# Twelve small table loads move from ScalarE's DMA queue to SyncE's, behind the pieces of the first modulation

## The chip, the cores and the metric

The kernel runs on one core of a Trainium2 chip. The metric is the device time of one execution, in microseconds (us). The engines are TensorE (PE, with its weight load PEld), VectorE (DVE), ScalarE (ACT), GpSimd (POOL) and SyncE (SP). SP and ACT both issue DMA transfers; the profile shows the issuing instructions as SPq and ACTq. Each engine works through its own instructions strictly in program order.

## The reference, cut to what matters

The program is one inference step of a trunk of two layers over 128 context tokens and 512 latent tokens (five tiles of 128), with a model width of 1024, all in float32:

```python
for l in range(DEPTH):                       # DEPTH = 2
    sh1, sc1, gt1, sh2, sc2, gt2 = split(silu(cond) @ w_ada[l] + b_ada[l], 6)   # for context and latents
    h = rms_norm(x, norm_mix_pre[l]) * (1 + sc1) + sh1
    y = even_mixer(h) if l % 2 == 0 else mla_mixer(h)
    x = x + gt1 * rms_norm(y, norm_mix_post[l])
    ...                                      # squared-ReLU MLP with sh2, sc2, gt2 in the same way
```

Layer 0 is the even mixer: one wide projection `w_in`, then gated linear attention heads and retention heads. The gates are

```python
gate_pre = einsum('bldr,drk->bldk', gk_lr, w_gk2) + b_gk2     # from 2 x 16 columns of the projection
log_a = log_sigmoid(gate_pre) / 16
b = cumsum(log_a within a chunk of 64)                        # positions and a triangle matrix
```

## The kernel before, in words

**Order.** No instruction is placed by hand. Every piece of work is a Python generator (a thread). A planner, `Weave`, keeps a clock for each engine with estimated costs, and each time it gives an engine the ready instruction of the most urgent thread; the resulting order is the program. So an edit of one thread can change the order of the instructions around it on all engines. A number that a thread yields is a pause on the planner's clock, and an `Event` a wait for another thread. `w.aside(...)` issues several loads and goes on.

**Waits of loads.** A load signals its landing on one of eight semaphores (`DMAHW0` to `DMAHW7` in the listings below), which the loads of SP and ACT take in turn. A load waits on its engine until the load before it on the same semaphore has landed. It also waits until its destination is free.

**The start.** `prepare` loads the condition (`cc`, 16 rows) and the identity on SP, and the biases and norms (`vec`, `post`) and the matrix `fold` on ACT. From `cc`, ACT and DVE make silu(cond): an exponential on ACT (`e<-cc`), then a reciprocal and a product on DVE. TensorE transposes it to `cT`, and DVE copies it into `wide`, the stationary operand of all modulation matmuls.

`ada_first` makes the first shift and scale of layer 0 in four quarters of 256 columns each. SP loads their weights as pieces `rada` in an order that `FIRST_LOADS` gives, mixed with the five tiles of `x` and the first four quarters (along the input width) of the first group of `w_in`, `raw` (480 columns). The pieces of the first two quarters are 128x4x256 (0.52 MB each, four to a quarter); those of the last two are 128x2x256 (0.26 MB, eight to a quarter) and take slots of the pools `sv` and `sg`, which the mixer uses later. For each quarter TensorE multiplies the pieces by `wide` into `ps`, ACT copies the sums to `row`, four small matmuls with `fold` turn them, and DVE makes `mod` from them. When all pieces of the four quarters are issued, the event `self.loaded` is set. Three things wait for it: the further weights of `w_in`, the modulation pieces of the next sections (128x512, 0.26 MB), and a part of `make_tables`.

`pre_norm` makes, for every tile and quarter, `xn`, its transposes into a PSUM bank (`ps`), `h` = scale and shift (half on DVE, half on ACT), and `hT` in two parts for the matmuls (ACT's cast and DVE's difference). `gemm_first` multiplies all tiles by the first group of columns of `w_in` (`pg<-wh,hT` and so on), quarter after quarter as they come. `gemm_nat` then goes through the further groups; the second one has 256 columns, and its weights are `wp`.

**`make_tables`** loads what the gates need: the weights and biases of the gates (`wf`, zeroed first by POOL; six loads of 16x4x64 and four of 1x4x64), the positions (`pos`), and the triangle tables (`dist`, 128x256). From them ACT makes `wg` (two casts, with a difference on DVE) and `tri`, and sets `tables`, for which each tile's thread waits after its first group of columns. After `self.loaded` it loads the masks, the decay rates (`lg`, `lgs`) and what else the retention heads need.

All instructions go through one helper line, so the profile names line 271 for all of them; the tiles tell them apart.

Of the kernel before, what the change touches and what calls it, by code (L numbers as in the profile page):

```python
# [33 lines left out]
C_ID, C_TF, C_TB, C_DF, C_DB, C_MF, C_MB, C_DT, C_COS, C_SIN, C_POS, C_FOLD = (  # L34
    0, 128, 256, 384, 512, 640, 768, 896, 1024, 1152, 1280, 1288)
# [298 lines left out]
class Trunk:  # L334
# [1195 lines left out]
    def even(self, ph, ready):  # L1530
        nc, io, w = self.nc, self.io, self.w
# [4 lines left out]
        con = io["consts"]  # L1536
        w.set(self.early, (sv, sg))
        tl = lambda nm, shape, dt=F32: pe.tile(shape, dt, tag=nm, name=nm)
        tri, pos = tl("tri", [P, 256], F32R), tl("pos", [P, 8])
# [11 lines left out]

        def make_tables():

            a = nc.scalar
            wf, hwf = yield from self.take(sg, [98, NH, 2, 64], F32, "wf")
            nc.gpsimd.memset(wf, 0.0)
            nc.gpsimd.memset(ones[96:98], 1.0)
            dist, hd = yield from self.take(sg, [P, 512], F32, "dist")

            loads = [lambda: a.dma_start(pos, con[:, C_POS:C_POS + 8]),  # L1560
                     lambda: a.dma_start(dist[:, 0:256], con[:, C_TF:C_TF + 256])]
            for d in range(2):
                for r in (0, 32, 64):
                    loads.append(lambda d=d, r=r: a.dma_start(
                        wf[r + d * 16:r + d * 16 + 16, :, d], io["w_gk2"][0, d].rearrange("r (h c) -> r h c", h=NH)))
                for r in (96, 97):
                    loads.append(lambda d=d, r=r: a.dma_start(
                        wf[r:r + 1, :, d], io["b_gk2"][0:1, d].rearrange("o (h c) -> o h c", h=NH)))
            there = Event()
            w.aside(*loads, then=lambda at: w.set(there, None, at))  # L1570
            yield there

            wf_ = wf.rearrange("p h d c -> p (h d c)")
            nc.scalar.copy(wg, wf_)
            nc.vector.tensor_sub(wg[64:98], wf_[64:98], wg[64:98].bitcast(F32))
            nc.scalar.copy(wg[96:97], wf_[96:97])
            self.drop(hwf)
            nc.scalar.copy(tri, dist[:, 0:256])
            nc.vector.tensor_copy(pos16, pos[:, 2:4])
            for s in gkT:  # L1580
                nc.vector.tensor_copy(s[96:98], ones[96:98])
            w.set(tables)
            yield self.loaded
            yield 2.0
            dt, hdt = yield from self.take(self.rows, [P, P], F32, "dt")
            e0, h0 = yield from self.take(self.rows, [P, P], F32, "e0")
            e1, h1 = yield from self.take(self.rows, [P, P], F32, "e1")
            nc.sync.dma_start(dist, con[:, C_DF:C_DF + 512])
            nc.vector.tensor_copy(masks, dist[:, 256:512].rearrange("p (a i) -> p a i", a=2))
            w.set(masked)  # L1590
            nc.sync.dma_start(rtab, con[:, C_COS:C_COS + 256].rearrange("p (a t c) -> p a t c", a=2, c=32))
            nc.sync.dma_start(gn, io["gla_norm"][0].partition_broadcast(P))
            nc.sync.dma_start(lg, io["ret_decay"].rearrange("o d h -> (o d h)").partition_broadcast(P))
            for d in range(2):
                nc.sync.dma_start(lgs[d * 64:d * 64 + 64], io["ret_decay"][0, d].partition_broadcast(64))
            nc.sync.dma_start(dt, con[:, C_DT:C_DT + P])
            w.set(gained)
            yield 20.0
            for s in (lg, lgs):
                nc.scalar.activation(s, s, AF.Exp)  # L1600
                nc.vector.tensor_scalar(s, s, -1.0, None, op0=ALU.mult)
            for h in range(NH):
                nc.scalar.activation(e0, dist[:, 0:128], AF.Exp, scale=lg[:, h:h + 1])
                nc.scalar.activation(e1, dist[:, 128:256], AF.Exp, scale=lg[:, 4 + h:5 + h])
                nc.vector.tensor_mul(e0, e0, dist[:, 256:384])
                nc.vector.tensor_mul(e1, e1, dist[:, 384:512])
                nc.vector.tensor_add(dmat[:, h], e0, e1)
                nc.scalar.activation(dec_t[:, h], dt, AF.Exp, scale=lgs[:, h:h + 1])
                yield 2.0
            nc.scalar.activation(dec128, lgs, AF.Exp, scale=128.0)  # L1610
            for d in range(2):
                nc.vector.tensor_scalar(kd[:, :, d], lg[:, d * 4:d * 4 + 4], pos[:, d:d + 1], None, op0=ALU.mult)
            nc.scalar.activation(kd, kd, AF.Exp)

            nc.vector.tensor_scalar(kd, kd, 0.125, None, op0=ALU.mult)
            nc.vector.tensor_scalar(dmat, dmat, 0.0625, None, op0=ALU.mult)
            self.drop(hd, hdt, h0, h1)
            w.set(tables2)

        tables2 = Event()  # L1620
        w.spawn(make_tables(), 0.0)
        G = [[Event() for _ in range(NT)] for _ in EVEN_GROUPS]
        kv_ev = {k: [Event() for _ in range(NT)] for k in ("gla", "ret")}
# [800 lines left out]
```

## Time and profile before

| | before |
|---|---|
| median of 3 runs | 1512.07 us (1511.71 to 1513.47) |
| profiled execution, its own time | 1510.94 us |
| its span, first to last instruction | 1508.8 us |
| mean granted clock | 0.997 |
| TensorE busy | 1468.6 us, 97% of the span |
| ScalarE busy | 659.4 us, 44% |
| transfers | 171.45 MB, mean 114 GB/s; the first fortieth of the span 299 GB/s |

Rows of the timeline are: start, length (us), engine, line, operation, output and inputs, shapes, number of instructions; in brackets the engine's idle time before it and what ended it. A DMA row of ACTq or SPq is the time of the issuing instructions, not of the transfer; the time from issue to landing stands in rows of its own.

### The profile page before, as it was taken

What the parts mean: (1) busy time and instruction counts of PE and PEld (TensorE: products, weight loads), DVE (VectorE), ACT (ScalarE), POOL (GpSimd) and SP (SyncE); (2) the same over time, 40 slices, a digit from 0 to 9 for tenths busy, and PEclk for the clock granted to TensorE, in tenths of its full rate; (3) what the DMA queues carried; (4) which work ended last, traced back from release to release, by engine and by line L of the source; (5) the groups of instructions that cost most, each with busy time, mean ns of one, the idle gap of its engine ahead of it and who ended that gap; (6) DMA issues with size and microseconds to landing.
All of it is one profiled execution on the core that took longest, in us unless ns stands there. A gap on an engine that the chain in (4) does not pass through costs nothing.

```text
span 1508.8 us, 23115 instructions
## 1 busy us (share of the span) xinstructions
PE 1468.6 (97%) x8651; PEld 1304.4 (86%) x8651; DVE 1085.8 (72%) x2234; ACT 659.4 (44%) x1543; POOL 114.5 (8%) x133
## 2 busy tenths in 40 slices
PE   4899999999999999999999999999999999999997
PEld 1688888888899899899898899997889989988996
DVE  2663674657677777777869788884765869996777
ACT  3583533546432223223247476664654323332332
POOL 0000200100121121021020100000012000000000
PEclk9999999999999999999999999999999999999999
DMA  9656222143455454354414210113522223432332
GB/s 299 200 168 196 82 75 70 39 132 112 147 159 156 140 147 147 113 148 151 133 45 133 68 29 22 43 44 124 168 84 70 70 71 112 133 119 84 98 101 110
DMA packets 152400, 171.45 MB, mean 114 GB/s; under 512 B 12272, under 2 KB 100960, under 8 KB 152288
## 3 DMA queue, kind: packets, MB, share of 16 engines
q1 hardware_dynamic: 151104, 169.59, 36.6%
q8 instruction: 68, 1.11, 0.3%
q10 hardware_dynamic: 1184, 0.39, 0.1%
q14 instruction: 44, 0.36, 0.1%
HBM read 161.36 MB, written 8.59 MB: 113 GB/s over the span
## 4 chain that ended last, share of the span: by engine, by line
PE 93%; DVE 3%; ACT 2%; DMA 1%; issue 0%; SPq 0%; DVEq 0%; ACTq 0%
PE p L271 57%; PE pg L271 21%; PE ps L271 13%; PE pqk L271 2%; PE pv L271 1%; DMA rada<-in_w_ada 1%; DVE sm L271 0%; DVE y L271 0%; DVE rope L271 0%; DMA x<-in_x_prompt 0%; ACT junk L271 0%; DVE x L271 0%; DMA wf<-in_w_gk 0%; ACT sm L271 0%; ACT hT L271 0%
## 5 line engine op out<-in xcount | busy, mean ns | idle before, releaser
L271 PE MATMUL p<-wh,hid 128*128 128x512 f32 x1280 | 399.3, 390 | 0.0
L271 PEld LDWEIGHTS p<-wh,hid 128*128 128x128 f32 x1280 | 240.3, 188 | 49.4
L271 PE MATMUL p<-hT,wh 128*128 128x256 f32 (+1 forms) x1280 | 279.6, 309 | 0.0
L271 PE MATMUL p<-wl,hid 128*128 128x512 f32 x640 | 249.5, 390 | 0.0
L271 PE MATMUL pg<-wh,hT 128*128 128x512 f32 (+2 forms) x760 | 245.9, 399 | 1.2 <-ACT hT L271 0.9
L271 DVE TENSOR_TENSOR wl<-raw,wh 128x1024 fp32r<-128x1024 f32 (+2 forms) x137 | 165.3, 1209 | 76.0 <-ACT wh L271 70.8
L271 PEld LDWEIGHTS p<-hT,wh 128*128 128x128 f32 x1280 | 214.8, 188 | 0.8
L271 ACT CAST wh<-raw 128x1024 fp32r<-128x1024 f32 (+2 forms) x141 | 144.8, 1033 | 132.1 <-PE p L271 88.4
L271 PE MATMUL p<-hT,wl 128*128 128x256 f32 (+1 forms) x640 | 198.2, 310 | 0.0
L271 PEld LDWEIGHTS pg<-wh,hT 128*128 128x128 f32 x760 | 140.0, 189 | 31.2 <-issue 4.7
L271 DVE SCALAR_TENSOR_TENSOR ada<-rada,cT,ada 128x512 f32<-128x512 f32 x196 | 146.5, 777 | 0.0
L271 PEld LDWEIGHTS p<-wl,hid 128*128 128x128 f32 x640 | 120.2, 188 | 24.1
L271 DVE TENSOR_TENSOR y<-y,p 128x512 f32<-128x512 f32 x140 | 95.8, 685 | 58.4 <-PE p L271 57.7
L271 POOL TENSOR_TENSOR r<-r 128x384 f32<-128x384 f32 (+1 forms) x80 | 82.4, 1030 | 722.9 <-ACT hid L271 385.4
L271 PE MATMUL pg<-wl,hT 128*128 128x512 f32 (+2 forms) x320 | 130.5, 408 | 0.0
L271 PEld LDWEIGHTS p<-hT,wl 128*128 128x128 f32 x640 | 120.5, 188 | 0.0
L271 ACT ACTIVATE r<-p 128x384 f32<-128x384 f32 (+1 forms) x80 | 35.0, 438 | 152.5 <-PE p L271 152.5
L271 PE MATMUL p<-hT,wq 128*128 128x320 f32 x576 | 88.1, 310 | 0.0
L271 PEld LDWEIGHTS p<-hT,wq 128*128 128x128 f32 x576 | 85.5, 188 | 0.5
L271 DVE TENSOR_TENSOR hid<-r,hid 128x384 fp32r<-128x384 f32 (+1 forms) x80 | 38.9, 487 | 48.8 <-POOL r L271 48.7
L271 PEld LDWEIGHTS pg<-wl,hT 128*128 128x128 f32 x320 | 60.7, 190 | 15.2 <-issue 3.9
L271 ACT CAST wq<-tw 128x512 fp32r<-128x512 f32 x48 | 27.6, 618 | 71.4 <-DVE tw L271 58.1
(290 smaller groups left out, 2384.7 us busy)
## 6 DMA issues: line engine op xcount, KB each, us to landing
raw<-in_w_mlp SPq DMA_DIRECT2D x128, 512.0 KB, 4.1
rada<-in_w_ada SPq DMA_DIRECT2D x176, 256.0 KB, 3.4
raw<-in_w_in_even SPq DMA_DIRECT2D x16, 512.0 KB, 4.5
rada<-in_w_ada SPq DMA_DIRECT2D x8, 512.0 KB, 6.9
x<-in_x_sample SPq DMA_DIRECT2D x8, 512.0 KB, 5.9
gate<-gate SPq DMA_DIRECT2D x8, 512.0 KB, 4.3
raw<-in_w_out_even SPq DMA_DIRECT2D x8, 512.0 KB, 5.0
raw<-in_w_out_odd SPq DMA_DIRECT2D x8, 512.0 KB, 3.9
```

The source lines that it names most:

```text
L271: emit = lambda: real(*a, **k)
```

## The change

`make_tables` now begins with the wait for `self.loaded`, and its twelve first loads are issued by SP. Within them the ten loads of `wf` come first and `pos` and `dist` last; the later `yield self.loaded` is gone. `wf` and `dist` also take their slots only then.

```diff
         def make_tables():
 
-            a = nc.scalar
+            yield self.loaded
             wf, hwf = yield from self.take(sg, [98, NH, 2, 64], F32, "wf")
             nc.gpsimd.memset(wf, 0.0)
             nc.gpsimd.memset(ones[96:98], 1.0)
             dist, hd = yield from self.take(sg, [P, 512], F32, "dist")
 
-            loads = [lambda: a.dma_start(pos, con[:, C_POS:C_POS + 8]),
-                     lambda: a.dma_start(dist[:, 0:256], con[:, C_TF:C_TF + 256])]
+            a = nc.sync
+            loads = []
             for d in range(2):
                 for r in (0, 32, 64):
                     loads.append(lambda d=d, r=r: a.dma_start(
@@ ... @@
+            loads += [lambda: a.dma_start(pos, con[:, C_POS:C_POS + 8]),
+                      lambda: a.dma_start(dist[:, 0:256], con[:, C_TF:C_TF + 256])]
             there = Event()
             w.aside(*loads, then=lambda at: w.set(there, None, at))
             yield there
@@ ... @@
             w.set(tables)
-            yield self.loaded
             yield 2.0
```

What this does to the order, at three places. ScalarE, start of the program, before (`fold` is the last load of `prepare`, `e<-cc` the first arithmetic):

```order
L271 DMA fold<-in_consts 128x128
L271 DMA pos<-in_consts 128x8
L271 DMA dist_159<-in_consts 128x256
L271 DMA wf_154<-in_w_gk 16x4x64 x3
L271 DMA wf_154<-in_b_gk 1x4x64 x2
L271 DMA wf_154<-in_w_gk 16x4x64 x3
L271 DMA wf_154<-in_b_gk 1x4x64 x2
L271 ACTIVATE e_105<-cc_104 16x128
L271 ACTIVATE junk,sm_207<-x_170 128x1024
```

and now:

```order
L271 DMA post_107<-in_norm_mlp_post 16x128
L271 DMA fold<-in_consts 128x128
L271 ACTIVATE e_105<-cc_104 16x128
L271 ACTIVATE junk,sm_206<-x_166 128x1024
L271 ACTIVATE sm_206<-sm_206,eps 128x1
L271 ACTIVATE sm_206<-sm_206 128x1
L271 COPY row_256<-ps_193 128x256
```

The twelve loads between `fold` and `e` are gone. SyncE, from the last pieces of the fourth quarter (128x2x256) on, before, with the waits of each load (`raw` at the end are the weights of the second group of columns):

```order
L271 DMA rada_475<-in_w_ada 128x2x256 [waits DMAHW2_49]
L271 DMA rada_481<-in_w_ada 128x512 [waits DMAHW3_49]
L271 DMA rada_494<-in_w_ada 128x512 [waits DMAHW4_49]
L271 DMA rada_500<-in_w_ada 128x512 [waits DMAHW5_49]
L271 DMA rada_508<-in_w_ada 128x512 [waits DMAHW6_49]
L271 DMA dist_159<-in_consts 128x512 [waits DMAHW7_49,Activation_49]
L271 DMA raw_516<-in_w_in_even 128x2x256 [waits DMAHW0_49,DVE_49]
L271 DMA raw_526<-in_w_in_even 128x2x256 [waits DMAHW1_49,DVE_49]
L271 DMA raw_544<-in_w_in_even 128x2x256 [waits DMAHW2_49,DVE_49,Activation_49]
```

and now, from the last of the four 128x512 pieces on:

```order
L271 DMA rada_499<-in_w_ada 128x512 [waits DMAHW2_49]
L271 DMA wf_473<-in_w_gk 16x4x64 [waits DMAHW3_49,Pool_49]
L271 DMA wf_473<-in_w_gk 16x4x64 [waits DMAHW4_49]
L271 DMA wf_473<-in_w_gk 16x4x64 [waits DMAHW5_49]
L271 DMA wf_473<-in_b_gk 1x4x64 [waits DMAHW6_49]
L271 DMA wf_473<-in_b_gk 1x4x64 [waits DMAHW7_49]
L271 DMA wf_473<-in_w_gk 16x4x64 [waits DMAHW0_49]
L271 DMA wf_473<-in_w_gk 16x4x64 [waits DMAHW1_49]
L271 DMA wf_473<-in_w_gk 16x4x64 [waits DMAHW2_49]
L271 DMA wf_473<-in_b_gk 1x4x64 [waits DMAHW3_49]
L271 DMA wf_473<-in_b_gk 1x4x64 [waits DMAHW4_49]
L271 DMA pos<-in_consts 128x8 [waits DMAHW5_49]
```

The twelve loads (the last, `dist`, follows the last row shown) now stand between these pieces and the weights of the second group. ScalarE, from the copy of the fourth quarter's sums (`row<-ps`) on, before (`h_631` and `h_634` are the fourth quarter of the first tiles):

```order
L271 COPY row_589<-ps_532 128x256
L271 CAST hT_91<-h_578 128x256
L271 CAST hT_91<-h_580 128x256
L271 ACTIVATE h_598<-ps_591,mod_164,mod_165 128x128
L271 CAST hT_91<-h_598 128x256
L271 CAST wp_519<-raw_516 128x512
L271 ACTIVATE h_631<-ps_620,mod_164,mod_165 128x128
L271 CAST wp_575<-raw_526 128x512
L271 ACTIVATE h_634<-ps_621,mod_164,mod_165 128x128
L271 CAST hT_91<-h_631 128x256
```

and now (the fourth quarter of the first tiles is `h_634`, `h_636`, `h_638`):

```order
L271 COPY row_594<-ps_520 128x256
L271 ACTIVATE h_604<-ps_589,mod_160,mod_161 128x128
L271 CAST hT_91<-h_604 128x256
L271 CAST wg_153<-wf_473 98x512
L271 CAST wp_587<-raw_507 128x512
L271 CAST wp_592<-raw_588 128x512
L271 CAST wg_153<-wf_473 1x512
L271 ACTIVATE h_634<-ps_623,mod_160,mod_161 128x128
L271 ACTIVATE h_636<-ps_624,mod_160,mod_161 128x128
L271 CAST wp_600<-raw_593 128x512
L271 ACTIVATE h_638<-ps_625,mod_160,mod_161 128x128
L271 CAST tri<-dist_484 128x256
```

The casts of `wg` and `tri`, which stood among the first and second quarter's work, now stand ahead of and among the fourth quarter's `h`. The order of TensorE, VectorE, GpSimd and SyncE differs through the first half of layer 0 in the same way; from there to the end the instructions come in the same order as before, but for numbers of buffers.

## The prediction

> **What bounds the kernel now.** I read the page's sections 1 and 4 first, then the busy time by windows, then the timeline of the first 60 us, engine by engine. Sections 1 and 4: TensorE is busy for 97% of the span, and the chain that ended last is TensorE for 93% of it.
>
> ```profile
> span 1508.8 us, 23115 instructions
> PE 1468.6 (97%) x8651; PEld 1304.4 (86%) x8651; DVE 1085.8 (72%) x2234; ACT 659.4 (44%) x1543; POOL 114.5 (8%) x133
> PE 93%; DVE 3%; ACT 2%; DMA 1%; issue 0%; SPq 0%; DVEq 0%; ACTq 0%
> ```
>
> So 40 us of the span are TensorE's idle time. The windows (start:end, length, then busy us of PE, PEld, DVE, ACT, POOL, then granted clock, DMA share, GB/s) say where it lies.
>
> ```profile
> 0.00:5.00 5.00, 0.00 (x0) 0.00 (x0) 0.34 (x2) 1.28 (x1) 0.93 (x6) 1.00 0.45 121
> 5.00:10.00 5.00, 0.00 (x0) 0.00 (x0) 0.00 (x0) 0.00 (x0) 0.00 (x0) 1.00 0.86 281
> 10.00:15.00 5.00, 0.00 (x0) 0.00 (x0) 0.00 (x0) 0.00 (x0) 0.00 (x0) 1.00 0.96 306
> 15.00:20.00 5.00, 1.54 (x11) 0.92 (x15) 2.60 (x10) 1.84 (x5) 0.00 (x0) 1.00 0.82 252
> 20.00:25.00 5.00, 4.51 (x36) 1.33 (x26) 0.48 (x1) 0.78 (x2) 0.00 (x0) 1.00 1.03 347
> 25.00:30.00 5.00, 2.74 (x20) 1.27 (x21) 2.70 (x11) 4.06 (x10) 0.00 (x0) 1.00 1.06 375
> 30.00:35.00 5.00, 5.00 (x24) 2.39 (x17) 2.59 (x7) 2.46 (x6) 0.00 (x0) 1.00 1.08 386
> 35.00:40.00 5.00, 3.16 (x22) 2.07 (x22) 3.32 (x10) 3.76 (x9) 0.00 (x0) 1.00 0.60 206
> 40.00:45.00 5.00, 4.64 (x35) 2.68 (x34) 4.29 (x15) 3.29 (x11) 0.00 (x0) 1.00 0.65 199
> 45.00:50.00 5.00, 3.27 (x28) 1.61 (x26) 3.62 (x9) 4.16 (x11) 0.00 (x0) 1.00 0.86 270
> 55.00:60.00 5.00, 5.00 (x35) 3.83 (x34) 2.65 (x10) 3.07 (x8) 0.00 (x0) 1.00 0.46 146
> 200.00:300.00 100.00, 100.00 (x542) 83.03 (x541) 60.77 (x126) 43.63 (x79) 11.38 (x14) 1.00 0.18 53
> ```
>
> TensorE idles for 25 of the first 50 us, most of it before it starts at all; from 55 us on it has none for hundreds of us. What brings that point forward shortens the run by about as much, since the chain behind it is TensorE's own work. The timeline says why the start is late.
>
> ```profile
> 4.00 0.36 ACTq L271 DMA_DIRECT2D fold<-in_consts  x1
> 4.40 0.45 ACTq L271 DMA_DIRECT2D pos<-in_consts  x1
> 14.92 1.31 ACTq L271 DMA_DIRECT2D wf<-in_b_gk  x2
> 16.29 0.31 ACT L271 ACTIVATE e<-cc 16x128 f32<-16x128 f32 x1 [14.27 <-DMA wf<-in_w_gk]
> 19.39 1.94 PE L271 MATMUL ps<-rada,wide 128*32 128x256 f32 x16
> 23.08 1.08 PE L271 MATMUL ps<-rada,wide 128*32 128x256 f32 x8
> 24.23 0.37 ACT L271 COPY row<-ps 128x256 f32<-128x256 f32 x1 [6.03 <-PE ps L271]
> ```
>
> ScalarE (ACT) issues its loads itself, one behind the other, and its first arithmetic, the exponential of the condition (`e<-cc`), stands behind all of them. From 4.40 to 16.23 it is occupied with the twelve loads that the change takes away. Without `e` there is no `cT`, without `cT` no `wide`, and without `wide` no matmul of the modulation (19.39).
>
> **The change part by part.** *The start.* With the twelve loads gone, ACT is free at 4.36, and `e` can begin 11.9 us earlier. The first modulation matmul comes 19.39 − 16.29 = 3.1 us behind it: 7.5 us. But the weights must be there. Up to the last piece of the first quarter, SyncE's queue (SP) brings the identity (0.07 MB), four pieces and one tile of x (0.52 MB each): 2.69 MB. By 5 us 0.6 MB had moved; the other 2.08 MB at 281 GB/s take 7.4 us, so the piece lands at 12.4. A group of four matmuls behind it (1.08) and the copy of the sums to `row` stands at 13.6, against 24.23: 10.6 us earlier. At best it is the full 11.9. At worst the fourth piece, whose issue ended in the trace at 8.3, has the longest landing of its kind:
>
> ```profile
> 5.98 2.34 SPq L271 DMA_DIRECT2D rada<-in_w_ada  x3
> DMA to landing us min/median/max: 2.9/5.5/7.7
> DMA to landing us min/median/max: 3.6/4.0/5.5
> ```
>
> (the first such line is for the modulation pieces up to 60 us, the second for `wf`). That gives 16.0, the copy at 17.2, and 7.0 us. I take 10.6, by the rate that the same queue showed in that stretch.
>
> *Three casts leave the head of ACT.*
>
> ```profile
> 31.97 0.60 ACT L271 CAST wg<-wf 98x512 fp32r<-98x512 f32 x1
> 38.12 0.61 ACT L271 CAST wg<-wf 1x512 fp32r<-1x512 f32 x1
> 39.16 0.40 ACT L271 CAST tri<-dist 128x256 fp32r<-128x256 f32 x1
> ```
>
> The first stood in a gap; the second was directly ahead of the next copy to `row`, the third ahead of the squares of the last tile. Gain 0 to 1.6; I take the 1.0 of the latter two.
>
> *Does the stream keep pace?* Until the last piece of the third quarter 7.77 MB more are needed (8 + 4 halves of a MB in pieces and x, three units of `w_in_even`). At the 369 GB/s of 20 to 35 us that is 21.0 us, landing at 33.4. TensorE used it here:
>
> ```profile
> 46.65 0.64 PE L271 MATMUL ps<-rada,wide 128*32 128x256 f32 x8
> 55.36 0.64 PE L271 MATMUL ps<-rada,wide 128*32 128x256 f32 x8
> 83.19 0.36 PE L271 MATMUL pg<-wp,hT 128*128 128x256 f32 x1
> ```
>
> and now wants it 11.6 earlier, at 35.0: in time. At 306 GB/s it lands at 37.8, 2.8 late. Loss 0 to 2.8; I take 0.5, since 347 to 386 were reached once the queue was full. The last piece of the fourth quarter (2.85 MB on) lands at 41.1 and is wanted at 44.
>
> *What the twelve loads cost on SP.* They stand behind four pieces of the next modulation and ahead of the weights of the second group of output columns. By the order each of them waits for the load eight places before, so the last four of the twelve go out only as the first four land. The four pieces (1.05 MB) have landed at about 44; loads nine to twelve are issued at 44 to 46, and the last of `wf` is there at 49 (4.0, the median). The three weight loads follow by 47.3 and land by 52, taking for them
>
> ```profile
> raw<-in_w_in_even SPq DMA_DIRECT2D x16, 512.0 KB, 4.5
> 50.22 0.62 ACT L271 CAST wp<-raw 128x512 fp32r<-128x512 f32 x1
> 49.87 0.47 ACT L271 ACTIVATE h<-ps,mod,mod 128x128 f32<-128x128 f32 x1
> 65.73 6.32 PE pg L271 x28
> ```
>
> On ACT the cast of `wg`, two casts of these weights and the small cast stand ahead of the last quarter's `h`: two `h` are done at 53.2. They free the banks of PSUM that TensorE needs for the last two tiles' transposes. It comes there 23 matmuls (0.226 each, from the 28 in 6.32), a dozen transposes and the small fold behind the last piece, 7 us after 44.9, at 51.9. So it waits 1.3; I take 1.5. Nothing if the weights land in 3 us; 4.5 if both rounds of landings take the 5.5 that was the longest of `wf`. [...]
>
> At nothing I cost SP's own issue time, twelve times some 0.45 (as `pos` above): from 55 us on the queue is far ahead of TensorE's need (55:60 shows 146 GB/s). That cover goes if the loads of the second group come later than TensorE's first use, 83.19 less the gain. `wf`'s memset on POOL now waits for a slot that a used piece leaves; POOL has nothing else there. The later tables (masks, `lg`, `dt`) are pushed back on SP as well, but their first use on ACT leaves SP until about 78 us to bring them, 30 us behind the twelve loads:
>
> ```profile
> 88.12 0.24 ACT L271 ACTIVATE lg<-lg 128x8 f32<-128x8 f32 x1
> ```
>
> *Sum.* −10.6 − 1.0 + 0.5 + 1.5 = −9.6 us. From 83.19 on the trace shows TensorE without a pause, and from the middle of the first layer the order of all engines is again the same, so I carry all of it to the end: span 1499.2, and with the 2.1 us around it 1501.3 for the profiled execution, which stood 1.1 below the median. Against the median: 1502.5.
>
> **The rivals.** *The stream is the bound and does not move faster.* By 50 us the windows moved 13.7 MB, and the head needs 13.3 and ACT's 0.4: at the old pace the last piece lands at 50, only 5.4 before its old use at 55.36. With the stall that is −4: 1508. For it: 1.0 and more of DMA share at 20 to 35. Against it: 206 and 199 GB/s at 35 to 45, when SP waited for rooms that engines still held, and these now come free earlier:
>
> ```profile
> SPq L271 <- DVE sm L271: 4.4, 1, 4.4
> SPq L271 <- PE ps L271: 4.1, 3, 2.4
> ```
>
> *TensorE starts early but slow.* The same kind of matmul took twice as long early on, though the clock column says 1.00 throughout:
>
> ```profile
> 30.57 0.77 PE L271 MATMUL pg<-wh,hT 128*128 128x480 f32 x1
> 36.18 0.38 PE L271 MATMUL pg<-wl,hT 128*128 128x480 f32 x1
> ```
>
> If it waits for pieces between 8 and 33 us it may stay slow until then: five groups at 1.08 for 0.64 (2.2) and 18 matmuls at twice 0.226 (4.1), less the 3.9 that it idled from 35 to 50: 2.4 lost, 1505. [...]
>
> *The loads block ACT from their new place, and the kernel is slower.* On ACT the twelve took 11.8 us. If they take that on SP from 44 us on, the weights behind them land at 61, the `h` are done at 63.8 and TensorE stands for 11.9: sum +0.8, 1513; with landings of 5.5 for 4.0 it is 16.3 and +5.3, 1517. It decides from a stall of 11.1 us. Against it: on ACT the loads shared the engines with 300 GB/s; behind the last pieces there is 146.
>
> **How the numbers follow.** The forecast has 0.60, the bound stream 0.13 (1508), the slow start 0.12 (1505), the blocked ACT 0.06 (1515), and 0.09 is for a loss by the new order that eats the gain down to less than 3 us. Faster by over 0.2% (3 us, about what can be told here) is then 0.85, within it 0.09, slower 0.06. All bounds together would span 1498.5 (11.9 + 1.6) to 1517; without the last two cases it is 1498.5 to 1508.5.
>
> **What would show it.** In the profile after: `e<-cc` at about 4.5; the copy to `row` at 13 to 14; the first matmul of the second group (`pg<-wp`) at 73 to 74 where it was 83.19; a wait of ACT ahead of `wg<-wf` of some 4 us and a pause of TensorE of one or two near 52. I am wrong if the copy to `row` comes after 17, if TensorE's pause near 52 is over 5, or if the matmul of the second group moves by 10 and the span does not.

## The result, and the profile after

The changed kernel took 1502.38 us (median; 1501.10 to 1502.76), the kernel before, beside it, 1512.77 us (1511.71 to 1513.62): a ratio of 0.9930, with a 95% interval of 0.9916 to 0.9944. The forecast was 1502.5, within 1498.5 to 1508.5. The profiled execution took 1501.1 us. Sections 1 and 4 of its page, which answer to the two lines shown of before:

```profile
span 1499.3 us, 23109 instructions
PE 1470.5 (98%) x8651; PEld 1305.1 (87%) x8651; DVE 1086.4 (72%) x2234; ACT 661.3 (44%) x1543; POOL 114.6 (8%) x133
PE 93%; DVE 3%; ACT 2%; DMA 1%; issue 1%; SPq 0%; DVEq 0%; ACTq 0%
```

TensorE's idle time (span less PE) fell from 40.2 to 28.8 us, by 11.4; its busy time rose by 1.9, with as many matmuls. So the span is 9.5 shorter. Both parts need an explanation. The busy time by windows, in the same columns as before:

```profile
5.00:10.00 5.00, 3.09 (x19) 0.95 (x19) 2.19 (x9) 1.65 (x4) 0.00 (x0) 1.00 1.04 360
10.00:15.00 5.00, 3.79 (x22) 1.62 (x22) 0.38 (x2) 1.54 (x4) 0.00 (x0) 1.00 1.07 370
15.00:20.00 5.00, 2.48 (x18) 0.70 (x18) 3.46 (x11) 3.97 (x11) 0.00 (x0) 1.00 1.09 355
30.00:35.00 5.00, 5.00 (x32) 2.79 (x31) 4.08 (x13) 4.06 (x10) 0.00 (x0) 0.70 1.09 382
```

TensorE now works from 5 us on. The stream moves 355 to 370 GB/s where it had moved 252 to 306: not only ACT but also SP became free (up to 60 us it had waited 7.2 us for landings of `wf`, and now for none). In 30 to 35 the granted clock is 0.70, where before it was 1.00: it stood at half from 29.62 to 33.03. The timeline of the head (ACT, then PE and SP):

```profile
3.77 0.31 ACT L271 ACTIVATE e<-cc 16x128 f32<-16x128 f32 x1 [1.75 <-DMA ident<-in_consts]
13.43 0.37 ACT L271 COPY row<-ps 128x256 f32<-128x256 f32 x1 [4.50 <-PE ps L271]
48.81 0.62 ACT L271 CAST wg<-wf 98x512 fp32r<-98x512 f32 x1
51.85 0.81 ACT L271 ACTIVATE h<-ps,mod,mod 128x128 f32<-128x128 f32 x2
```

```profile
6.43 1.08 PE L271 MATMUL ps<-rada,wide 128*32 128x256 f32 x8 [0.48 <-DVE wide L271]
12.28 1.08 PE L271 MATMUL ps<-rada,wide 128*32 128x256 f32 x8 [0.17 <-DMA rada<-in_w_ada]
45.99 0.64 PE L271 MATMUL ps<-rada,wide 128*32 128x256 f32 x8
53.01 0.27 PE L271 MATMUL ps<-ident,xn 128*128 128x128 f32 x1
67.86 0.28 PE L271 MATMUL pg<-wp,hT 128*128 128x256 f32 x1
```

```profile
39.31 2.00 SPq L271 DMA_DIRECT2D wf<-in_w_gk  x3
44.66 1.30 SPq L271 DMA_DIRECT2D wf<-in_b_gk  x2
46.55 0.36 SPq L271 DMA_DIRECT2D dist<-in_consts  x1
47.01 8.04 SPq L271 DMA_DIRECT2D raw<-in_w_in_even  x6
```

The exponential stands 12.5 us earlier than before (16.29), the first modulation group 13.0 (19.39), the copy to `row` 10.8 (24.23). The twelve loads take SP 7.6 us (39.31 to 46.91). `wg` is cast without a wait, and TensorE comes to the transposes at 53.01 without one.

**A mark for the head.** The first matmul of `pg<-wp` stands 15.3 earlier, but some of the work that stood ahead of it now stands behind it. A mark that has the same work ahead of it in both kernels is the first matmul of layer 0's MLP, with 1970 matmuls ahead in both (the window before counts the mark itself too). Before, then after, the time up to that mark as one window:

```profile
0.00:357.90 357.90, 332.38 (x1971) 263.44 (x1971) 203.06 (x457) 178.98 (x398) 27.32 (x41) 1.00 0.44 140
```

```profile
0.00:345.85 345.85, 332.36 (x1970) 262.99 (x1971) 203.29 (x457) 180.64 (x398) 27.36 (x41) 1.00 0.45 145
```

The head became 12.05 us shorter, all of it idle time of TensorE (25.52 to 13.49). What TensorE waited for up to 55 us, before and then after (us in total, times, longest):

```profile
PE ps L271 <- DMA wf<-in_w_gk: 18.2, 1, 18.2
PE ps L271 <- ACT row L271: 3.5, 3, 1.8
PE pg L271 <- ACT hT L271: 0.9, 2, 0.6
```

```profile
PE ps L271 <- DVE cc L271: 5.7, 1, 5.7
PE ps L271 <- DMA rada<-in_w_ada: 1.7, 4, 0.7
PE ps L271 <- ACT row L271: 1.6, 2, 1.1
```

**What was given back.** From the mark to the last matmul (1500.57 before, 1490.71 after) there are 1142.67 us before and 1144.86 after: 2.19 more, with the same work. Behind the last matmul it is 8.23 and 8.59. So −12.05 + 2.19 + 0.36 = −9.5, the span. Most of the 2.19 is in one place, where MLP 0 ends and the odd layer begins. The windows there (before, then after) are cut where the granted clock changes:

```profile
817.18:820.59 3.41, 1.25 (x8) 0.86 (x7) 3.41 (x11) 3.38 (x14) 0.00 (x0) 1.00 0.32 87
820.59:824.00 3.41, 3.41 (x16) 3.38 (x17) 3.35 (x14) 2.40 (x6) 0.00 (x0) 0.50 0.58 228
824.00:827.41 3.41, 3.41 (x30) 3.41 (x29) 3.11 (x8) 1.92 (x5) 0.00 (x0) 1.00 0.43 113
```

```profile
804.45:807.86 3.41, 1.70 (x9) 1.21 (x9) 3.41 (x9) 3.41 (x13) 0.00 (x0) 1.00 0.54 192
807.86:811.27 3.41, 2.64 (x13) 2.61 (x14) 3.34 (x14) 2.37 (x6) 0.00 (x0) 0.50 0.72 244
811.27:814.68 3.41, 3.41 (x18) 3.41 (x18) 2.28 (x6) 2.52 (x6) 0.00 (x0) 0.50 0.26 18
```

In both kernels TensorE has a thin stretch there, and its clock then falls to half: for 3.41 us before, for twice as long after (from 814.68 on it is 1.00 again). An extra 3.41 us at half clock, with TensorE busy throughout, is worth 1.7 us of work (an estimate: half of 3.41). Whether that is a result of the change is asked below.

### The profile page after: what moved, and what is told of

It is laid out like the page before. It is cut to its first block, busy times and chain, and to the rows that moved or that the text cites. A ratio compares the mean times of both kernels' runs of the same rounds, so it can differ in the third digit from the quotient of the medians.

```text
span 1499.3 us, 23109 instructions
## 1 busy us (share of the span) xinstructions
PE 1470.5 (98%) x8651; PEld 1305.1 (87%) x8651; DVE 1086.4 (72%) x2234; ACT 661.3 (44%) x1543; POOL 114.6 (8%) x133
## 3 DMA queue, kind: packets, MB, share of 16 engines
HBM read 161.36 MB, written 8.59 MB: 113 GB/s over the span
## 4 chain that ended last, share of the span: by engine, by line
PE 93%; DVE 3%; ACT 2%; DMA 1%; issue 1%; SPq 0%; DVEq 0%; ACTq 0%
PE p L271 57%; PE pg L271 20%; PE ps L271 13%; PE pqk L271 2%; PE pv L271 1%; DMA rada<-in_w_ada 1%; DVE y L271 0%; DVE rope L271 0%; DMA kr<-in_state_ret 0%; DVE sm L271 0%; DVE x L271 0%; SPq L271 0%; ACT junk L271 0%; ACT la L271 0%; DMA gate<-gate 0%
```

## The experiments

Theory A is the prediction's: ACT issues in order, so the loads held up the exponential and with it TensorE, and the first pieces of the weights are the second condition. Rival B: the small loads slow SP's stream, whichever engine's time they take. Rival C: the gain is in the later place of the three casts. All kernels are changes of the changed kernel's `make_tables`, unless said otherwise. The table has them all. "Mark" is the start of the MLP of layer 0 in the profiled execution, "rest" the time from there to the last matmul, "half" how long the clock stood at half near 810 us.

| kernel | loads: queue, place | median us (range) | ratio to before, 95% | first group | mark | rest | half |
|---|---|---|---|---|---|---|---|
| before | ACT, start | 1512.77 (1511.71–1513.62) | | 19.39 | 357.90 | 1142.67 | 3.41 |
| after | SP, late | 1502.38 (1501.10–1502.76) | 0.9930 [0.9916, 0.9944] | 6.43 | 345.85 | 1144.86 | 6.83 |
| r_after (the same) | SP, late | 1499.87 (1498.47–1500.11) | 0.9914 [0.9900, 0.9928] | 6.53 | 345.16 | 1144.51 | 6.83 |
| e1_place | ACT, late | 1504.04 (1503.49–1504.66) | 0.9945 [0.9928, 0.9961] | 6.46 | 350.64 | 1143.23 | 3.41 |
| e2_queue | SP, start | 1504.83 (1504.50–1506.11) | 0.9951 [0.9937, 0.9966] | 13.58 | 351.20 | 1143.47 | 3.41 |
| e3_pool | POOL, start | 1499.98 (1499.14–1500.33) | 0.9917 [0.9902, 0.9932] | 6.52 | 345.39 | 1143.28 | 3.41 |
| r_pool (the same) | POOL, start | 1500.02 (1499.53–1500.82) | 0.9915 [0.9902, 0.9929] | 6.51 | 346.10 | 1144.24 | 6.83 |
| e5_pool_late | POOL, late | 1501.03 (1498.96–1502.02) | 0.9924 [0.9910, 0.9937] | 6.53 | 347.25 | 1144.64 | 6.83 |
| e4_cond | ACT, behind `e` | 1514.62 (1513.41–1516.45) | 1.0014 [1.0005, 1.0023] | 6.48 | 363.01 | 1142.14 | 3.41 |
| e4b_cond | the same, without `dist` | 1504.32 (1503.64–1507.14) | 0.9951 [0.9938, 0.9963] | 6.55 | 352.08 | 1144.91 | 6.83 |
| e8_five | five on ACT at the start | 1503.80 (1502.82–1505.56) | 0.9949 [0.9936, 0.9961] | 10.80 | 349.93 | 1144.40 | 6.83 |
| e6_warm | SP, late, extra matmuls | 1501.08 (1498.98–1501.49) | 0.9926 [0.9914, 0.9939] | 6.49 | 345.88 | 1144.62 | 6.83 |
| e7_pool_warm | POOL, start, extra matmuls | 1500.27 (1498.90–1500.99) | 0.9922 [0.9910, 0.9935] | 6.76 | 346.64 | 1142.93 | 3.41 |
| e10_double | SP, late, loads twice | 1498.04 (1497.13–1500.57) | 0.9906 [0.9893, 0.9920] | 6.55 | 348.07 | 1142.50 | 3.41 |

**The place alone (e1_place).**

```diff
-            a = nc.sync
+            a = nc.scalar
```

> The twelve loads stay on ScalarE's queue and only their place changes, behind the pieces of the first shift and scale. Theory A (ScalarE issues in order, so what stands behind the loads waits for them: at the start the exponential of the condition, and with it TensorE): the start is that of the changed kernel, row copied at 13.4 us; but now the third quarter's copy to row, at 38.5 us in the changed kernel, stands behind the loads, which take 7.6 us (as on SP) to 11.8 us (as at the start), so TensorE pauses 7 to 11 us near 40 to 50, and the time is 1502.4 + 7 to 11 = 1509 to 1513. Rival B (the start became faster because SP's queue no longer shares semaphores with the small loads; ScalarE hardly matters): the loads disturb SP only once the stream is nearly done, 1502 to 1505. Rival C (the gain is in the later place of the three casts): 1502 to 1503.

Measured: 1504.04, with the start of the changed kernel (row at 13.57) and ACT occupied from 37.23 on:

```profile
37.23 0.72 ACTq L271 DMA_DIRECT2D wf<-in_w_gk  x1
46.40 0.37 ACT L271 COPY row<-ps 128x256 f32<-128x256 f32 x1 [8.10 <-DMA wf<-in_b_gk]
```

```profile
46.83 0.39 PE L271 MATMUL ps<-fold,row 128*128 128x4 f32 x2 [2.29 <-ACT row L271]
49.70 1.08 PE L271 MATMUL ps<-rada,wide 128*32 128x256 f32 x8 [1.50 <-issue]
```

Theory A's wait is there, 9.1 us of ACT and a copy to `row` 7.9 later than in the changed kernel. But TensorE had matmuls of the first group in hand until 44.5, so it paused 3.8 us, not 7 to 11; with a stretch of half clock behind the pause (6.83 us from 49.1 on) the mark comes 4.8 to 5.5 later. The mechanism holds and the size was wrong: I had counted ACT's hold as TensorE's pause. The time by itself lies in rival B's interval (1502 to 1505) and not in A's, and it does not exclude rival C either; what speaks for A here is the pause, in the place that only A gave for it.

**The queue alone (e2_queue).** The wait for `self.loaded` goes back to its old line, so SP issues the loads at the start:

```diff
-            yield self.loaded
             wf, hwf = yield from self.take(sg, [98, NH, 2, 64], F32, "wf")
...
             w.set(tables)
+            yield self.loaded
             yield 2.0
```

> The twelve loads go to SyncE's queue but stay at the start of the program, ahead of the first piece of w_ada. Theory A in its full form (TensorE starts with the later of the condition and the first pieces): the exponential is at 3.8 us, but the first piece is issued 7.6 to 11.8 us later than at 1.95, so the first copy to row is at 21 to 25 us where the changed kernel has 13.4 and the kernel before 24.2; most of the gain is lost, 1509 to 1513. Rival D (it is the exponential alone that sets the start): row at 13 to 15 us, 1502 to 1504.

Measured: 1504.83; the exponential at 4.28, and the first group only here:

```profile
13.58 1.08 PE L271 MATMUL ps<-rada,wide 128*32 128x256 f32 x8 [6.13 <-DMA rada<-in_w_ada]
```

The copy to `row` is at 21.30, as theory A said, and the exponential alone is not enough (rival D is out). But the time is 4 us better than A's interval: the mark is 6.7 us earlier than before, with the copy to `row` only 2.9 earlier. The copy to `row` was too early a place to read the gain off; the first modulation group, 5.8 earlier, is nearer to it.

**GpSimd's queue (e3_pool, e5_pool_late, r_pool).** e3_pool is e2_queue with `a = nc.gpsimd`; e5_pool_late is the changed kernel with it; r_pool is e3_pool again.

> The twelve loads go to GpSimd's queue at the start of the program. Theory A (neither ScalarE nor SyncE is held up): exponential at 3.8 us, row at 13.4 to 14.5 us (0.4 MB more in the stream ahead of it at most), no loads on SP at 39 us; 1501 to 1503.5, the same as the changed kernel within what can be told. Rival B (small loads beside the stream make SP wait for shared semaphores, whoever issues them): the stream from 5 to 20 us falls back to 250 to 306 GB/s, row at 16 to 20 us, 1506 to 1510.

> The loads stand where the changed kernel has them, behind the pieces of the first shift and scale, but GpSimd's queue issues them in place of SyncE's. If the 7.6 us of SyncE's issuing at 39 us cost nothing, because the stream is far ahead of TensorE by then: 1501.5 to 1503.5, the changed kernel's time. If they cost the 1.5 us that the prediction put on them: 1500 to 1501.5. If GpSimd's place at the start is what makes the kernel with GpSimd's queue 2.4 us faster than the changed one: 1501.5 to 1503.5 here too, and if it is the queue: 1499.5 to 1500.5.

> The kernel with the twelve loads on GpSimd's queue at the start once more, beside the changed kernel. If it is faster by what the first comparison said: 1499.5 to 1500.5 and some 2 us less than the changed kernel. If that was the spread between jobs: within 1 us of it.

Measured: 1499.98 and 1500.02 with the loads at the start, 1501.03 with them late, 1499.87 for the changed kernel in the same rounds as r_pool. So the 2.4 us by which e3_pool seemed to beat the changed kernel was the spread between sets of runs: the same changed kernel gave 1502.38 in one and 1499.87 in the other. Three ways of keeping the loads off ACT and off the start of SP give the same time within what can be told. In e3_pool the three casts stand early (`tri` at 23.76), and the mark is at 345.39: rival C is out. That GpSimd's loads go ahead of the pieces costs the first of them a little (the second group at 9.68, 8.90 in the changed kernel), and the copy to `row` stands at 15.30: later than I had it under theory A (13.4 to 14.5), while the time is below A's interval and far from rival B's (1506 to 1510).

e5_pool_late's 1501.03 lies in the interval that I had set for a cost of 1.5 us on SP, but that interval was counted from 1502.38, and the changed kernel gave 1499.87 as well. By the ratios to before, e5_pool_late (0.9924) is no faster than the changed kernel (0.9930 and 0.9914). Its mark is 1.4 to 2.1 later, and 0.9 to 1.5 of that is there at the copy to `row` already (14.92), ahead of the loads. So no run shows a cost of SP's 7.6 us of issuing in the changed kernel.

**ACT, but behind the exponential (e4_cond, e4b_cond).** e4_cond is e2_queue with `a = nc.scalar` and a `yield self.prepared` (the event that the condition is ready) as its first line. In e4b_cond the load of `dist`, with the cast of `tri`, goes behind `self.loaded`, and SP issues it.

> The loads stay on ScalarE's queue near the start, but behind the exponential of the condition. Theory A: the exponential is at 3.8 us and TensorE's first modulation matmul at 6.4 as in the changed kernel; ScalarE is then occupied from 4.1 to about 16, so its squares (7.2) and the copy to row (13.4) come at 16 to 18: of the 10 us some 3 to 5 are lost, 1505 to 1508. If the exponential alone mattered (rival D): 1502 to 1503. Rival B (shared semaphores slow SP's stream to 250 to 306 GB/s from 5 to 20 us): row at 18 to 24, 1508 to 1513.

Measured: 1514.62, slower than before by 0.14% and above all three intervals. The exponential and the first group are as early as expected (3.82 and 6.48), but ACT does not come out of its loads:

```profile
27.81 0.33 ACTq L271 DMA_DIRECT2D dist<-in_consts  x1
```

```profile
29.65 1.02 PE L271 MATMUL ps<-fold,row 128*128 128x4 f32 x4 [15.15 <-ACT row L271]
```

The previous load on ACT, `pos`, had gone out at 15.20. In the order, `dist` waits for the semaphore `DMAHW2`, which a load of `w_in` on SP had used last; SP issued that at 19.56, behind all the pieces that stand ahead of it in SP's order. So ACT stood 12 us (15.56 to 27.81) for a load of the other queue.

> The loads on ScalarE's queue behind the exponential of the condition, as in the kernel that took 1514.6 us, but without the load of the triangle (`dist`), which goes to SyncE's queue behind the pieces. If that one load is what made the other kernel slow (it waited for a semaphore that a late load of SyncE's stream had before it, and held ScalarE from 15.6 to 27.8 us): ScalarE is free at about 15.6 us, row at 16 to 17, and 1504.5 to 1507.5. If every load beside the stream does it: row after 24 and 1510 or more.

Measured: 1504.32, just below that.

```profile
15.17 1.06 ACT L271 ACTIVATE junk<-x 128x1024 bf16<-128x1024 f32 x1 [10.97 <-DMA wf<-in_w_gk]
16.23 0.35 ACT L271 COPY row<-ps 128x256 f32<-128x256 f32 x1
```

One load of 131 KB was worth about 10 us: 10.3 by the medians, 9.5 by the ratios to before, 10.9 at the mark. The rest is theory A (ACT held until 15.1, row 2.8 late), and rival B in part: with the loads on ACT beside the stream it moved this much from 5 to 20 us (before, e4b_cond, e3_pool, and e8_five of the next part, with five loads on ACT):

```profile
5.00:20.00 15.00, 1.54 (x11) 0.92 (x15) 2.60 (x10) 1.84 (x5) 0.00 (x0) 1.00 0.88 280
```

```profile
5.00:20.00 15.00, 7.58 (x49) 2.76 (x49) 3.61 (x17) 3.41 (x10) 0.00 (x0) 1.00 0.90 295
```

```profile
5.00:20.00 15.00, 8.05 (x49) 2.77 (x49) 4.99 (x18) 5.64 (x14) 2.98 (x6) 1.00 1.06 353
```

```profile
5.00:20.00 15.00, 7.61 (x49) 2.96 (x49) 4.20 (x15) 4.22 (x12) 0.00 (x0) 1.00 1.01 342
```

280 to 295 GB/s with all the loads on ACT, 353 with them on GpSimd, 342 with five on ACT, and 361 and 357 over the same 15 us in the changed kernel's two profiles, with none. In the orders, ACT's and SP's loads share eight semaphores, and GpSimd's have their own (`DMASW0` and on). In the kernel before, SP's issuing waited 3.7 us for loads of `w_gk` and 3.5 us for one of `b_gk`, all on ACT's queue; in the changed kernel it waited for none. So B's mechanism exists, but these runs show it only where SP's stream and the small loads share semaphores. How much of the 12 us it carries was not separated: no run had ACT and SP's issuing both free and the stream slow. The nearest is the next run, in which the stream is close to its full rate and the exponential is late.

**How late may the exponential be (e8_five).** `pos`, `dist` and three loads of `wf` on ACT at the start, the other seven on SP behind `self.loaded` (the edit, cut, with comments added):

```diff
-            yield self.loaded
...
+            w.aside(*loads)            # pos, dist and three of wf, on nc.scalar
+            yield self.loaded
-            w.aside(*loads, then=lambda at: w.set(there, None, at))
+            w.aside(*late, then=lambda at: w.set(there, None, at))      # seven of wf, on nc.sync
```

> Five of the twelve loads (positions, triangle, three of wf) stay on ScalarE's queue at the start, ahead of the exponential; the other seven are on SyncE's queue as in the changed kernel. In the kernel before, these five ended at 8.1 us, so the exponential comes at about 8.2 us in place of 3.8. Theory A, with the pieces as the second condition: TensorE's first group at 10.8 us, four groups of 1.08 without a wait, row at 15.2 us in place of 13.4, and the time 1.8 us longer at most: 1502.5 to 1504.3. Rival L (every us of the exponential's delay costs a us, 5 of 12 loads costing 5/12 of the 10 us): 1506 to 1507.

```profile
8.14 0.31 ACT L271 ACTIVATE e<-cc 16x128 f32<-16x128 f32 x1 [6.12 <-DMA wf<-in_w_gk]
16.88 0.37 ACT L271 COPY row<-ps 128x256 f32<-128x256 f32 x1 [6.83 <-PE ps L271]
```

The time, 1503.80, lies in A's interval, but with the changed kernel at 1502.38 in one set and 1499.87 in another that is weak. The head says something else: the exponential is 4.4 us later than in the changed kernel, the first group 4.3 to 4.4, and the mark 4.1 to 4.8. Nearly every us of the exponential's delay cost a us, as rival L had it (though L's time, 1506 to 1507, was missed), and that with the stream at 342 GB/s; the pieces gave no cushion.

**TensorE's slow start (e6_warm, e7_pool_warm).** Matmuls that nobody reads, in the changed kernel and in e3_pool (the edit, cut, with comments added):

```diff
+            for _ in range(11):        # ahead of the transposes of cc
+                nc.tensor.matmul(ps, self.junk[:, 0:P], self.junk[:, 0:512], start=True, stop=True)
             yield arrived
...
+                for _ in range(4):     # ahead of each group of the first two quarters
+                    nc.tensor.matmul(fb[:, 0:256], self.junk[:, 0:P], self.junk[:, 0:256], start=True, stop=True)
                 got, held = yield evs[q, k0, sec]
```

> The changed kernel with matmuls added that nobody reads (on a zeroed tile): 11 of 512 columns before the transposes of the condition, and four of 256 columns ahead of each of the first eight groups of the modulation. They fill TensorE's pauses at the start, so that it is at its full rate before 22.8 us, where the changed kernel reaches it, and does not fall back at 29.6 us. Theory W (the slow clock in the head costs time): groups of eight matmuls at 0.64 in place of 1.08 us, no half clock from 29.6 to 33.0 us, 1499 to 1501. Rival S (the stream of pieces sets the head, and what a faster TensorE saves turns into waits for pieces): busy time falls and idle time rises by the same, 1502 to 1503.5.

> The same added matmuls, in the kernel that issues the twelve loads on GpSimd's queue at the start (1500.0 us). It has no half clock at 30 us, so only the start up to 23 us can gain. Theory W: 1498 to 1499.3. Rival S: 1499.5 to 1501.

Measured: 1501.08 and 1500.27, which can't be told from the kernels without them. In e6_warm:

```profile
6.49 0.64 PE L271 MATMUL ps<-rada,wide 128*32 128x256 f32 x8
43.85 0.64 PE L271 MATMUL ps<-rada,wide 128*32 128x256 f32 x8
52.74 0.33 PE L271 MATMUL ps<-ident,xn 128*128 128x128 f32 x1 [1.71 <-ACT h L271]
```

```profile
47.81 0.62 ACT L271 CAST wg<-wf 98x512 fp32r<-98x512 f32 x1 [1.05 <-DMA pos<-in_consts]
50.24 1.32 ACT L271 CAST wp<-raw 128x512 fp32r<-128x512 f32 x2 [1.81 <-DMA raw<-in_w_in_even]
```

The groups are fast (0.64 for 1.08), there is no half clock near 30, and the last piece is used at 43.85, 2.1 us earlier than in the changed kernel (1.6 earlier than in its second profile). Then TensorE waits 1.71 us at 52.74, for an `h` that stands behind the casts of `wg` and `wp` on ACT, which now wait for their loads. That is the prediction's last term, at its place and in its size. The mark is at 345.88, where it was. So neither of my two expectations had it: the slow start did cost some 2 us, and a wait that it had covered took them back. e7_pool_warm's time lies in rival S's interval; it has no such late loads, but fell to half clock twice in the head (9.1 to 12.5 and 22.8 to 26.2), so it doesn't test this cleanly.

**SP's share doubled (e10_double).**

```diff
-            w.aside(*loads, then=lambda at: w.set(there, None, at))
+            w.aside(*loads, *loads, then=lambda at: w.set(there, None, at))
```

> The changed kernel with the twelve loads issued twice on SyncE's queue, with the same data. If SyncE's time there is free because the next weights are needed only at 67.9 us: 1501.5 to 1503.5. The twelve took 7.6 us; another 7.6 to 12 push the weights of the second group from 47 to 55 us to 55 to 67, and their casts and first matmul to 61 to 73. If that is past the cover, TensorE pauses by 1 to 5 us near 68 and the time is 1503.5 to 1507.

```profile
63.43 0.29 PE L271 MATMUL ps<-ident,gk 128*96 128x128 f32 x1 [2.40 <-DVE gk L271]
```

The head shows the end of the cover: a pause of 2.4 at 63 us with a stretch of half clock behind it (64.92 to 68.33), and a mark at 348.07, 2.2 to 2.9 later. So in the head 7.6 us of SP cost nothing and another 8 cost 2 to 3. But the time did not rise: 1498.04, below both intervals, against 1499.87 for the changed kernel in the same rounds. In the profiled execution (1500.57, the slowest of the four) the clock stood at half for 3.41 us near 810 and not for 6.83, which returns 1.7 us (an estimate: half of 3.41); why the other three were still 2 to 3.4 us faster, no trace shows. It stays open.

**The changed kernel again (r_after).**

> The changed kernel once more, unaltered, so that it stands beside the next kernels on the same chip in the same rounds: 1501 to 1503. Its profile also shows what differs from execution to execution: if the stretches at half clock (3.4 us at 30, 6.8 us at 808) come from this kernel's pauses alone, they stand there again with the same length; if their length also depends on where the pauses fall in a fixed beat of 3.4 us, it may be 3.4 or 6.8.

Measured: 1499.87, below what I expected of it. The stretches at half clock are not the same: 17.24 to 24.07 in the head, where the first profile had 29.62 to 33.03, and 805.72 to 812.55. e3_pool and r_pool, one program in two executions, differ near 807 as before and after do (e3_pool, then r_pool):

```profile
807.44:810.85 3.41, 2.73 (x13) 2.70 (x14) 3.34 (x14) 2.38 (x5) 0.00 (x0) 0.50 0.69 245
810.85:814.26 3.41, 3.41 (x30) 3.41 (x30) 3.41 (x9) 2.43 (x6) 0.00 (x0) 1.00 0.25 33
```

```profile
806.17:809.58 3.41, 2.58 (x8) 1.85 (x9) 3.41 (x13) 2.89 (x10) 0.00 (x0) 0.50 0.48 137
809.58:812.99 3.41, 3.41 (x18) 3.41 (x17) 3.07 (x10) 2.48 (x5) 0.00 (x0) 0.50 0.35 141
```

So the second stretch comes and goes without any change of the program. It stood in both profiles of the changed kernel, and before was profiled only once, so that the change makes it likelier is not excluded. The table's last two columns say what it costs: where the clock stood at half for 3.41 us the rest took 1142.1 to 1143.5 us, where for 6.83 us 1144.2 to 1144.9, and the two means are 1.7 apart.

## Why the prediction was right, point by point

**What bounds the kernel.** Right: TensorE's late start, and all of the gain is idle time ahead of 55 us.

**The start, −10.6.** Right at the place it was worked out for: the copy to `row` at 13.43 (13.6 forecast), 10.8 earlier, in the second profile at 14.02. The reason given, that the weights must be there first, holds at this place too: TensorE's last group of the first quarter began at 12.28, where a wait for its piece ended (forecast 12.4). The rate was not the one assumed (360 GB/s and not 281), but by the windows some 3.3 MB had moved by then, and not only the 2.69 that I counted. What was wrong is to read the head's gain off the copy to `row`: TensorE's waits for pieces add up to only 1.7 us, and the head followed the exponential (12.5 earlier, mark 12.05 and 12.7 earlier). e8_five shows the same slope from the other side. e2_queue shows that the pieces do bind when they are 7 us late.

**The casts, −1.0, and the stream, +0.5.** Mis-sized, in the same direction: TensorE's waits for `row` fell from 3.5 to 1.6, those for `hT` from 0.9 to nothing, and the stream was not late at the third quarter. Together with the next term, I had +1.0 behind the copy to `row`, and the head shows −1.25.

**The loads on SP, +1.5.** Nothing in the changed kernel, where I had expected ACT to wait some 4 us ahead of `wg` and TensorE near 52. The times on SP were right (the loads issued until 46.91, the weights behind them from 47.01), and the landing was shorter: the last loads of `wf` were issued by 45.96 and there at 48.81, within 2.9 us (the six loads of 16 KB have a median of 3.3, against 4.0 on ACT). No wait stood ahead of `wg` or of the transposes. From 40 to 50 us the transfers moved 188 and 139 GB/s, against 380 in the 20 us ahead. But TensorE was later than I had it: the last piece was used at 45.99, not at 44.9, and the transposes came at 53.01, not at 51.9, when the `h` were done. e6_warm makes TensorE 2.1 us earlier, and the stall is there with 1.71. So the wait exists, and in the changed kernel another term covered it, the slow TensorE, that I had kept apart as a rival: the two don't add, the later of them counts.

**Carried to the end.** This step failed: of the 12.05, 2.5 did not reach the end, 1.7 of it (an estimate: half of 3.41) by a second stretch of half clock, which comes and goes between executions of one program (e3_pool, r_pool). Its premise was a misreading: from 83.19 on the trace of before is not without a pause. TensorE was busy for 1.25 of the 3.41 us from 817.18, and a half clock followed.

**The sum.** −9.6 forecast, −9.5 in the profiled execution, but as −12.05 and +2.55. In the second set of runs the same kernel was 2.5 us faster. That the median came out at the forecast to 0.1 is chance; the range, 1498.5 to 1508.5, is what the terms supported.

**The rivals.** The stream now moves at a share of 1.04 to 1.09 from 5 us to 40, and bound little (the 1.7 us of waits for pieces). The slow start was there (1.08 a group up to 19.29, half clock from 29.6 to 33.0), about as long as before: the trace's clock records begin at 35.53 before and at 22.79 after, where the time of a group falls from 1.08 to 0.64, 16.1 and 16.4 us behind the first group. Ahead of that the column's 1.00 has no record behind it. That it stays slow while it waits for pieces was my estimate; with the pauses filled (e6_warm) a group took 0.64 from 6.49 on. By e6_warm the slow start is worth some 2 us, which hide the stall of the term above, so that taking it away alone gains nothing. The loads did not block ACT. `pg<-wp` came at 67.86 and not at 73 to 74, because one of three modulation groups and some of the gates' work moved behind it.

## What to carry to other kernels

In this kernel small loads on the queue of an engine that also computes held up what stood behind them, and at the worst place, the first arithmetic of the program (`e` at 16.29 for 3.77): twelve loads of 0.24 MB together were worth 0.7 to 0.9% of a 1.5 ms kernel; another place alone or SP's queue alone recovered more than half of it, GpSimd's queue all. Look also at what such a load shares with another queue: one load of 131 KB that waited for a semaphore of the other queue's stream held its engine for 12 us. And measure a head at a mark behind which the work is the same in both kernels, not at the first row that moves.

## What the runs showed of the hardware

The half clock came in a fixed beat. In all 14 profiled executions the stretches at 0.50, up to the end of TensorE's work, are 3.41 us or 6.83 us long, and in the six executions that have more than one they begin on the same beat of 3.413 us (in the changed kernel 29.62 and 807.86 are 228 beats apart), while the beat's place differs between executions. So a thin stretch of TensorE could cost up to 1.7 or 3.4 us here by chance (an estimate: half of 3.41 and 6.83), and differences of 2 us between two kernels of this kind can be that alone, by the same estimate. How empty a stretch must be for the fall is not settled here: TensorE had been busy for 1.25 of the 3.41 us ahead of the fall near 820 in the kernel before, and for 1.70, 1.69 and 1.61 near 807 in the changed kernel, e3_pool and r_pool. So a beat that is half empty was enough in these. It was not enough each time: in the kernel before, the beat from 35.53 on had 1.82, and no fall followed.
